# A matmul kernel whose TensorE, VectorE and ScalarE first jump past the end of their programs and back

**Chip, cores, metric.** One core of one Trainium2 chip. The time is the device time of an execution in microseconds; smaller is better. Every execution quoted here was of the fast state by the test that compares runs of one kernel. The experiments ran in three calls on three chips, so each ratio is to the runs of the kernel before in the same call.

## The reference

```python
def reference(x, weight, sub_value):          # x 16 x 512 x 1024, weight 1024 x 768, all float32
    return (np.matmul(x, weight) - sub_value).astype(np.float32)
```

As rows, x is 8192 x 1024: 64 tiles of 128 rows. The core must move 87.03 MB: x, the weights and sub_value in, the result out.

## The kernel before

SyncE issues all transfers in an order fixed by a list. ScalarE casts a tile of x to half precision; the tile is transposed by TensorE (then ScalarE copies it out of PSUM) or, for 18 of 64 tiles, by VectorE; TensorE multiplies with the resident weights; VectorE subtracts sub_value, and the result goes out. TensorE's program is a straight head of four tiles and a loop of ten times six tiles. The other engines run straight through. The parts that matter here:

```python
TRANSFERS = [
    ('x', 0, 1), ('w', 0, 1), ('x', 1, 1), ('w', 1, 1), ...          # cut
    ('s', 48, 8), ('x', 56, 8), ('o', 24, 8), ('o', 32, 8), ('s', 56, 8),
    ('o', 40, 8), ('o', 48, 8), ('o', 56, 5), ('o', 61, 2), ('o', 63, 1),
]
...
    dve.add(lambda: nc.vector.memset(idle_w, 0.0), then=count("idle"))
    dve.add(lambda: nc.vector.memset(idle_x, 0.0), then=count("idle"))
...
    def idle(n):                                     # dummy matmuls, ahead of the first transpose
        pe.add(lambda: nc.tensor.ldweights(idle_w, tile_position=(0, 0)), [(counter["idle"], 2)])
        for _ in range(n):
            pe.add(lambda: loaded_matmul(po_b[:, NPO - 1, 0], idle_w, idle_x, start=True, stop=True))
...
    idle(13)
    cast(0)
    ...                                              # one more dummy, then the first real work:
    transpose_tile(0)
...
    for q in (sp, act, dve, pool):
        q.emit(q.ops)
    if LOOP:
        first, size, times = LOOP                    # (4, 6, 10)
        pe.emit(pe.ops[: marks[first]])
        ends = [marks[first + size * n] for n in range(times + 1)]
        pe.emit_loop([pe.ops[a:b] for a, b in zip(ends, ends[1:])])
        pe.emit(pe.ops[ends[-1] :])
```

## Time and profile before

| | before |
|---|---|
| time, median of the 3 runs that were there at the start | 210.81 us (210.66 to 210.87) |
| span of the profiled run, first to last instruction | 208.9 us |
| TensorE: first dummy, first transpose, end of the last matmul | 1.47, 7.42, 201.65 us |
| last output (384 KB): issue, landing | 202.67, 207.64 us |
| 16 DMA engines on the data queue | 97.9% of the span |

The span is split between two resources that are both nearly full, TensorE (busy for 94% of it) and the DMA engines (97.9%); which of them sets the end is the question of this study. Ends of matmuls are modelled in the profile. The lines that carry the reading stand in the prediction. One view that the prediction did not use is the table of issues (size in KB, then us from issue to landing). Its last three outputs are:

```profile
out_dram<-so_ring SPq DMA_DIRECT2D x1, 1920.0 KB, 10.5
out_dram<-so_ring SPq DMA_DIRECT2D x1, 768.0 KB, 6.6
out_dram<-so_ring SPq DMA_DIRECT2D x1, 384.0 KB, 5.0
```

Note the 5.0 us of the smallest; what it says becomes clear with the experiments.

### The profile page before, as it was taken

What the parts mean: (1) busy time and instruction counts of PE and PEld (TensorE: products, weight loads), DVE (VectorE), ACT (ScalarE), POOL (GpSimd) and SP (SyncE); (2) the same over time, 40 slices, a digit from 0 to 9 for tenths busy, and PEclk for the clock granted to TensorE, in tenths of its full rate; (3) what the DMA queues carried; (4) which work ended last, traced back from release to release, by engine and by line L of the source; (5) the groups of instructions that cost most, each with busy time, mean ns of one, the idle gap of its engine ahead of it and who ended that gap; (6) DMA issues with size and microseconds to landing.
All of it is one profiled execution on the core that took longest, in us unless ns stands there. A gap on an engine that the chain in (4) does not pass through costs nothing.

```text
span 208.9 us, 2609 instructions
## 1 busy us (share of the span) xinstructions
PE 196.8 (94%) x1234; PEld 75.5 (36%) x700; DVE 127.1 (61%) x218; ACT 108.8 (52%) x113; POOL 0.8 (0%) x7
## 2 busy tenths in 40 slices
PE   7999699979999999999999999999999999999960
PEld 0233244323434433443443443443344344334310
DVE  0233235956894795597399389479739938942330
ACT  2555659506673761844645576184574746516300
POOL 1000000000000000000000000000000000000000
PEclk9999999999999999999999999999999999999996
DMA  6999999999999999999999999999999999999993
GB/s 199 420 427 425 435 420 437 436 412 447 425 445 433 419 433 423 452 433 414 445 439 408 442 419 447 430 452 406 438 442 419 428 428 433 433 433 423 418 416 136
DMA packets 5476, 87.08 MB, mean 417 GB/s; under 512 B 608, under 2 KB 608, under 8 KB 1888
## 3 DMA queue, kind: packets, MB, share of 16 engines
q1 hardware_dynamic: 5472, 87.03, 97.9%
q8 instruction: 1, 0.02, 0.0%
q14 instruction: 3, 0.02, 0.0%
HBM read 61.87 MB, written 25.17 MB: 417 GB/s over the span
## 4 chain that ended last, share of the span: by engine, by line
PE 72%; DMA 19%; SPq 4%; ACT 1%; issue 1%; DVE 0%
PE po_b L181 64%; DMA x_ring<-in_x_dram 19%; PE pt_b L318 7%; SPq L281 3%; SPq L245 1%; ACT xt_b L331 0%; DVE so_ring L400 0%; ACT x_b L300 0%; SPq L542 0%; ACT x16p_b L300 0%; SPq L133 0%
## 5 line engine op out<-in xcount | busy, mean ns | idle before, releaser
L181 PE MATMUL po_b<-w_sb,xt_b 128*128 128x384 f16 x704 | 126.0, 326 | 0.5 <-DVE w_sb L248 0.3
L400 DVE TENSOR_TENSOR so_ring<-po_b,so_ring 128x768 f32<-128x768 f32 x64 | 60.6, 956 | 58.3 <-PE po_b L181 39.3
L331 ACT COPY xt_b<-pt_b 128x1024 f16<-128x1024 f16 x44 | 44.5, 1012 | 67.2 <-PE pt_b L318 66.3
L351 DVE STREAM_TRANSPOSE xtp_b<-x16p_b 32x256 f32<-32x256 f32 x144 | 62.7, 435 | 3.2 <-ACT x16p_b L300 1.1
L181 PE MATMUL po_b<-w_sb,xtp_b 128*128 128x384 f16 x320 | 61.3, 326 | 1.3 <-DVE xtp_b L351 1.1
L380 PEld LDWEIGHTS <-xt_b 128*128 128x128 f16 x352 | 34.5, 98 | 58.0 <-issue 54.0
L300 ACT CAST x_b<-x_ring 128x1024 f16<-128x1024 f32 x46 | 47.2, 1048 | 4.0 <-DMA x_ring<-in_x_dram 4.0
L318 PE MATMUL pt_b<-ident,x_b 128*128 128x128 f32 x184 | 47.6, 274 | 1.6 <-ACT x_b L300 1.5
L318 PEld LDWEIGHTS pt_b<-ident,x_b 128*128 128x128 f32 x184 | 25.5, 141 | 46.3 <-issue 36.1
L300 ACT CAST x16p_b<-x_ring 128x1024 f16<-128x1024 f32 x18 | 18.8, 1046 | 14.3 <-DMA x_ring<-in_x_dram 14.3
L380 PEld LDWEIGHTS <-xtp_b 128*128 128x128 f16 x160 | 15.7, 98 | 19.8 <-issue 17.7
L248 DVE CAST w_sb<-so_ring 128x768 f16<-128x768 f32 x8 | 4.1, 556 | 13.1 <-DMA so_ring<-in_weight_dram 13.1
L181 PE MATMUL po_b<-idle_x,idle_w 128*128 128x512 f16 x26 | 9.2, 514 | 1.5 <-DVE idle_x L411 1.5
L331 ACT COPY xtp_b<-pt_b 128x1024 f16<-128x1024 f16 x2 | 2.0, 1012 | 2.3 <-PE pt_b L318 2.3
L300 ACT ACT_TABLE_LOAD x1 | 1.3, 1283 | 0.9 <-SPq L133 0.9
L415 PEld LDWEIGHTS <-idle_w 128*128 128x128 f16 x4 | 0.4, 100 | 1.5 <-DVE idle_x L411 1.5
L410 DVE MEMSET idle_w<- 128x64 uint32 x1 | 0.1, 112 | 1.0 <-SPq L133 1.0
L487 ACT CAST stub<-ident 128x1 f16<-128x1 f32 x2 | 0.4, 195 | 0.0
L170 POOL TENSOR_SCALAR_AFFINE_SELECT ident<-ident 128x128 f32<-128x128 f32 x1 | 0.3, 292 | 0.1
L411 DVE MEMSET idle_x<- 128x256 uint32 x1 | 0.3, 272 | 0.0
L169 POOL MEMSET ident<- 128x128 f32 x1 | 0.2, 204 | 0.5 <-SPq L133 0.5
L464 POOL MEMSET mark<- 128x1 f32 x1 | 0.1, 98 | 24.2 <-ACT xtp_b L331 24.2
(4 smaller groups left out, 0.4 us busy)
## 6 DMA issues: line engine op xcount, KB each, us to landing
so_ring<-in_sub_value_dram SPq DMA_DIRECT2D x7, 3072.0 KB, 24.3
out_dram<-so_ring SPq DMA_DIRECT2D x7, 3072.0 KB, 26.1
x_ring<-in_x_dram SPq DMA_DIRECT2D x5, 4096.0 KB, 23.0
x_ring<-in_x_dram SPq DMA_DIRECT2D x2, 2048.0 KB, 27.6
so_ring<-in_weight_dram SPq DMA_DIRECT2D x4, 768.0 KB, 8.7
x_ring<-in_x_dram SPq DMA_DIRECT2D x1, 3072.0 KB, 28.8
x_ring<-in_x_dram SPq DMA_DIRECT2D x2, 1024.0 KB, 25.2
out_dram<-so_ring SPq DMA_DIRECT2D x1, 1920.0 KB, 10.5
```

Source lines behind the costliest of these rows:

```text
L181: return nc.tensor.add_instruction(mybir.InstMatmult(name=nc.get_next_instruction_name(), engine=full.engine, ins=list(full.ins), outs=lis ...
L245: sp.add(lambda st=st, at=at: nc.sync.dma_start(out=st, in_=w_c[at]), then=(sem, 16))
L248: lambda at=at, r=r, st=st: nc.vector.tensor_copy(out=w_sb[:, at, r], in_=st[:, r]),
L281: sp.add(lambda here=here, there=there: nc.sync.dma_start(out=here, in_=there), waits, (sem, 16))
L300: act.add(lambda: nc.scalar.copy(out=to, in_=x_in), waits, count("cast"))
L318: pe.add(lambda: nc.tensor.transpose(words, from_, ident), waits, count("turn") if last else None)
L331: act.add(lambda: nc.scalar.copy(out=to, in_=pt_b[:, b]), waits, count("evac"))
L351: dve.add(lambda: nc.vector.transpose(xt[b * Q : (b + 1) * Q, :, a * Q : (a + 1) * Q], x16[a * Q : (a + 1) * Q, :, b * Q : (b + 1) * Q],), ...
L380: pe.add(lambda weights=weights: nc.tensor.ldweights(weights, tile_position=(0, 0)), [w for w in waits if w[0] in ready])
L400: dve.add(lambda: nc.vector.tensor_tensor(out=o, in0=po[:, :, :NS], in1=o, op=mybir.AluOpType.subtract), [landed["s", mi], (counter["mul"] ...
L415: pe.add(lambda: nc.tensor.ldweights(idle_w, tile_position=(0, 0)), [(counter["idle"], 2)])
L487: lambda t=t: nc.scalar.copy(out=stub[:, t - n_mt : t - n_mt + 1], in_=ident[:, :1]), [(counter["ident"], 2)], count("cast")
```

## The change

The intent is to have the far end of each long program fetched at the start, instead of while the DMA engines are full of data: in the trace of before, one packet of instructions of 16 KB starts at 35.4 us and three of 8 KB at 57.0, 86.9 and 160.8 us. Three engines make a first turn in which they skip all their work and land behind it, then come back and do it.

```diff
-    for q in (sp, act, dve, pool):
+    engines = OrderedEngineSet([mybir.EngineType.PE, mybir.EngineType.DVE, mybir.EngineType.Activation])
+    for q in (sp, pool):
         q.emit(q.ops)
+    turn = nc.alloc_registers("turn", engines=engines)
+    nc.regs_mov(turn, 0)
+    nc.br("turn_head", engines=engines)
+    with nc.body("turn_head", valid_engines=engines):
+        nc.br_cmp(turn, 0, on_true="past", on_false="work", comp_op="IS_EQ", engines=engines)
+    with nc.body("work", valid_engines=engines):
+        for q in (act, dve):
+            q.emit(q.ops)
         ...                                # TensorE's head and loop, as before
+        nc.br("past", engines=engines)
+    with nc.body("past", valid_engines=engines):
+        nc.regs_alu(turn, turn, 1, op=mybir.AluOpType.add)
+        nc.br_cmp(turn, 2, on_true="turn_head", on_false="rest", comp_op="IS_LT", engines=engines)
+    nc.switch_bb("rest")
```

> **What bounds the kernel now.** I read the page first (busy shares, DMA queues, the chain), then the order of time around the start, then the gaps of TensorE up to 52 us, then a table by stretches.
>
> ```profile
> PE 196.8 (94%) x1234; PEld 75.5 (36%) x700; DVE 127.1 (61%) x218; ACT 108.8 (52%) x113; POOL 0.8 (0%) x7
> q8 instruction: 1, 0.02, 0.0%
> q14 instruction: 3, 0.02, 0.0%
> PE 72%; DMA 19%; SPq 4%; ACT 1%; issue 1%; DVE 0%
> ```
>
> TensorE is busy for 94% of the span, and the chain that ended last is 72% TensorE and 19% a DMA. The two queue lines are the whole traffic of instructions within the span: four packets. In the trace they start at 35.4 us (the one of 16 KB, 1.07 us long) and at 57.0, 86.9 and 160.8 us (8 KB each, 0.31 to 0.33 us).
>
> Where TensorE is the bound is told by stretches (width, then busy time of PE, PEld, DVE, ACT, POOL, clock, DMA share, GB/s):
>
> ```profile
> 26.07:44.77 18.70, 17.61 (x112) 6.79 (x64) 12.29 (x22) 11.05 (x12) 0.00 (x0) 1.00 1.00 426
> 96.80:201.50 104.70, 104.70 (x677) 41.78 (x385) 69.12 (x117) 55.02 (x58) 0.00 (x0) 1.00 1.00 431
> ```
>
> From 52 us to the last matmul TensorE has no idle time at all: 104.70 of 104.70 us. Before, it has. So a delay at the start costs what is left of it after TensorE's waits before 52 us. The start, in order of time (start, length, engine, operation, in brackets the idle time before and what ended it):
>
> ```profile
> 0.90 1.28 ACT L300 ACT_TABLE_LOAD   x1 [0.90 <-SPq L133]
> 1.14 0.27 DVE L411 MEMSET idle_x<- 128x256 uint32 x1
> 1.47 6.12 PE L181 MATMUL po_b<-idle_x,idle_w 128*128 128x512 f16 x14 [1.47 <-DVE idle_x L411]
> 4.96 1.04 ACT L300 CAST x_b<-x_ring 128x1024 f16<-128x1024 f32 x1 [2.77 <-DMA x_ring<-in_x_dram]
> 6.86 1.03 DVE L248 CAST w_sb<-so_ring 128x768 f16<-128x768 f32 x2 [5.44 <-DMA so_ring<-in_weight_dram]
> 7.42 0.60 PE L318 MATMUL pt_b<-ident,x_b 128*128 128x128 f32 x4
> ```
>
> ScalarE idles 2.77 us for the first x, VectorE 5.44 us for the first weights. TensorE does not idle: it fills 1.47 to 7.42 with 14 dummy matmuls, which wait for VectorE's second memset and stand in order ahead of the first transposes. The cast that those need ends at 4.96 + 1.04 = 6.00. So a later start of TensorE, or of VectorE's memsets, moves the transposes at 7.42 one for one; ScalarE's does not until it exceeds its own 2.77 us. These are the gaps after that:
>
> ```profile
> 18.63 2.11 PE L181 MATMUL po_b<-w_sb,xt_b 128*128 128x384 f16 x12 [0.32 <-DVE w_sb L248]
> 23.30 0.44 PE L318 MATMUL pt_b<-ident,x_b 128*128 128x128 f32 x2 [1.47 <-ACT x_b L300]
> 26.07 0.81 PE L181 MATMUL po_b<-w_sb,xtp_b 128*128 128x384 f16 x4 [0.16 <-DVE so_ring L400]
> 44.77 0.81 PE L181 MATMUL po_b<-w_sb,xtp_b 128*128 128x384 f16 x4 [1.09 <-DVE xtp_b L351]
> 51.16 0.81 PE L181 MATMUL po_b<-w_sb,xt_b 128*128 128x384 f16 x4 [0.15 <-ACT xt_b L331]
> ```
>
> A gap is slack only where what ended it does not itself follow TensorE. The following lines tell:
>
> ```profile
> 21.21 1.01 ACT L331 COPY xtp_b<-pt_b 128x1024 f16<-128x1024 f16 x1 [0.91 <-PE pt_b L318]
> 22.20 1.04 ACT L300 CAST x_b<-x_ring 128x1024 f16<-128x1024 f32 x1
> 25.05 2.69 DVE L400 TENSOR_TENSOR so_ring<-po_b,so_ring 128x768 f32<-128x768 f32 x3 [4.62 <-DMA so_ring<-in_sub_value_dram]
> 33.64 1.82 DVE L400 TENSOR_TENSOR so_ring<-po_b,so_ring 128x768 f32<-128x768 f32 x2 [5.90 <-DMA so_ring<-in_sub_value_dram]
> 49.07 1.04 ACT L300 CAST x16p_b<-x_ring 128x1024 f16<-128x1024 f32 x1 [7.60 <-DMA x_ring<-in_x_dram]
> ```
>
> The cast behind the 1.47 us gap stands right behind a copy at 21.21 that TensorE's own transposes released: that gap moves with TensorE and absorbs nothing. The others hang on transfers: 0.32 on the weights; 0.16 on VectorE's subtractions at 25.05, which waited for sub_value; 1.09 on VectorE's transposes, which follow without a break from 33.64, again a landing; 0.15 on the x that landed just before 49.07. Those transfers were issued long before (the x of 49 us at 10.35) and the DMA engines are full, so a start some us later does not move them. Slack: 0.32 + 0.16 + 1.09 + 0.15 = **1.72 us**.
>
> [...] no stall stands beside any of the four[...]. [...] In this trace a compare-and-branch of ScalarE has 33 ns and one of TensorE 174 ns, and the nine jumps back in TensorE's loop leave no gap after the first (whose 1.09 us VectorE explains)[...].
>
> **The change part by part.** It removes no work. Matmuls, casts, transfers, waits and TensorE's loop of ten bodies are the same, in the same order, by the comparison of the two programs. Per engine it adds, before the first useful instruction: one register move, a jump, a compare-and-branch taken to the far end, an add, a compare-and-branch back, a compare-and-branch not taken: six. At the end: an add and a compare-and-branch, at 202.6 us at the latest, while SyncE waits for the last transfers till 206.9; free. GpSimd and SyncE are not touched, so transfers start as before.
>
> (1) Sequencer work: 6 x about 0.1 us = 0.6 us, an estimate from the branch durations above.
>
> (2) Misses. The distances are 333 instructions on TensorE, 229 on VectorE, 157 on ScalarE[...]. The trace does not name the engine of a fetch packet[...]. One miss, estimated from this trace: from SyncE's issue of the first x at 0.94 to its first packet at 1.97 are 1.0 us; the packet itself 0.3 to 1.07 us[...]: about 2 us. TensorE's jumps may hit: its loop goes back 177 instructions after the fetch at 35.4 and no further fetch appears[...].
>
> (3) The delay d of TensorE's start is the larger of its own and VectorE's. No miss: d = 0.6. One: 2.6. Two: 4.6. ScalarE with two, its table load at 5.5, casts at 6.8, 1.8 later than before, but with TensorE's transposes as late as 12 us that is hidden.
>
> (4) Cost = d - 1.72 where positive: 0, 0.9, 2.9 us. At the tail it passes through, as the last matmul, the last subtraction (0.96 us) and the last 384 KB follow each other.
>
> (5) Gain: fetches in the span can move to the start, but none of the four stalls TensorE after 52 us. 0.
>
> I give no miss 0.3, one 0.3, two 0.35, more 0.05 (d about 7, cost 5): 0.27 + 1.0 + 0.25 = 1.5 as the mean. As part of a second miss lies under the clock of another engine's, I take 1.2 us: **212.0 us**.
>
> **Rivals.** *All hidden:* [...] for it speak the four packets alone and the loop's free jumps. Then 210.6 to 211.0 us. *Misses pile up:* [...] the fetch queues behind the x and weight transfers that SyncE has started meanwhile, and a miss takes 3 us; against it, the 16 KB packet under full DMA took 1.07 us. Then d is 7 to 8 and the time 216 us, over 2%. *The warmed end pays:* fetches of 0.3 us at 57, 87 and 161 us vanish[...]; against it, no stall in the bound stretch. Then 210.3 us. *ScalarE becomes the head's bound:* needs three misses there alone.
>
> **Range and chances.** 210.7 to 214.0 us holds the cases of no, one and two misses. Faster by over 2% would need 4.2 us saved where no wait on instructions is seen: 0.01. Slower by over 2% needs d above 5.9 us, three misses or more: 0.08. Within 2%: 0.91.
>
> **What the profile would show.** Step 1 and 2: the first dummy matmul at 1.5 + d, the table load at 0.9 + ScalarE's d, and instruction packets near 1 to 5 us. Step 3: the transposes at 7.42 + d, the first x cast still at about 4.96 unless ScalarE missed twice. Step 4: the gaps at 18.63, 26.07, 44.77 and 51.16 shrink by d together, and only the rest reappears as a later last matmul (201.65 before). I am wrong if the gap at 44.77 closes and the end yet stays, if the continuous stretch from 52 us gets gaps at fetches, or if the start moves by more than 6 us.

Passages on how instructions are fetched and how long a branch takes are cut from this prediction, as no trace or run of this case shows them. The sum itself stands as it was: 0.6 us of sequencer work and about 2 us a miss make d 0.6, 2.6 or 4.6 us, less 1.72 us of slack; the mean over the chances is 1.5 us, of which 1.2 were taken, on 210.8: 212.0 us. Three terms have lost ground to the cuts. Of the 0.1 us a step, what is left to rest on are the 33 and 174 ns of the trace, whose mean is 0.10. Of the 2 us a miss, a few tenths for waiting behind data are cut; 1.0 and 0.3 to 1.07 us are left, 1.3 to 2.1 together. And the count of misses, one on VectorE and perhaps one more on the way back, was the author's assumption: the trace of before did not show it.

## The result, and the profile after

The time did not change: 210.75 us median of 4 runs (210.46 to 211.06) against 210.84 us of before in the same session. The ratio is 0.9998, 95% interval 0.9980 to 1.0015. (Ratios here are the mean time of one kernel's fast runs over that of the other's in the same rounds, so not quite the ratio of the medians.) The result is correct.

Yet the start did move, by nearly what the prediction's case of "two misses" said. The order of time at the start of the changed kernel, to be held against the lines at 0.90, 1.14, 1.47, 4.96 and 7.42 us in the prediction:

```profile
1.77 1.28 ACT L300 ACT_TABLE_LOAD   x1 [1.77 <-issue]
5.63 0.11 DVE L410 MEMSET idle_w<- 128x64 uint32 x1 [5.63 <-issue]
5.91 1.04 ACT L300 CAST x_b<-x_ring 128x1024 f16<-128x1024 f32 x1 [2.85 <-DMA x_ring<-in_x_dram]
6.07 6.09 PE L181 MATMUL po_b<-idle_x,idle_w 128*128 128x512 f16 x14 [6.07 <-DVE idle_x L411]
12.00 0.60 PE L318 MATMUL pt_b<-ident,x_b 128*128 128x128 f32 x4
```

ScalarE is 0.87 us late, VectorE and, through its memsets, TensorE 4.60 us: 6.07 - 1.47. The sequencer records say which engine waited. The register move, jump, add and jump back run from 0.90 to 1.74 us on ScalarE and from 1.05 to 1.99 us on TensorE, without a hole. On VectorE the compare-and-branch starts at 1.04 us and the add behind it at 5.10: 4.06 us for one jump. The way back has no such hole (5.18 to 5.54). So one miss, on VectorE alone, and not two. (A jump is said to miss here if its engine's next sequencer record comes microseconds later and a packet of instructions lies in the hole, as the 8 KB at 3.25 us do here; what that packet brings is called the far page. The other jumps out and back in this trace, which are said to hit, have the next record 0.23 to 0.44 us after their start.)

The instruction packets have moved: in this trace they start at 2.04, 3.25 and 8.30 us (8 KB each) and 3.86 us (16 KB), and none is left later. Before, they were at 35.4, 57.0, 86.9 and 160.8 us.

Next, the gaps of TensorE. Of those that the prediction listed at 18.63, 23.30, 26.07, 44.77 and 51.16 us, one is still shown with a releaser (the view leaves out gaps under 0.15 us; the one of 26.07 is still there, 0.15 us before the matmul at 30.40):

```profile
27.65 0.44 PE L318 MATMUL pt_b<-ident,x_b 128*128 128x128 f32 x2 [1.40 <-ACT x_b L300]
```

That is the one said to move with TensorE; it did, by 4.34 us. Matmul by matmul, the lateness is 4.60 us at the first dummy, 4.10 after the weights' gap, 4.34 to 4.36 after ScalarE's chain, 2.99 after the gap of 44.77, 2.67 after that of 51.16, and 2.39 from 52.2 us to the last matmul. TensorE ends 2.39 us later, 204.04 for 201.65. The last subtraction of each kernel, before and after:

```profile
201.68 0.96 DVE L400 TENSOR_TENSOR so_ring<-po_b,so_ring 128x768 f32<-128x768 f32 x1 [1.64 <-PE po_b L181]
```

```profile
204.08 0.96 DVE L400 TENSOR_TENSOR so_ring<-po_b,so_ring 128x768 f32<-128x768 f32 x1 [1.64 <-PE po_b L181]
```

So 2.4 us of delay reach the last tile, and yet the time is the same. They vanish behind it, in the table of issues of the changed kernel:

```profile
out_dram<-so_ring SPq DMA_DIRECT2D x1, 1920.0 KB, 7.7
out_dram<-so_ring SPq DMA_DIRECT2D x1, 768.0 KB, 3.8
out_dram<-so_ring SPq DMA_DIRECT2D x1, 384.0 KB, 2.3
```

Each output is issued some 2.4 us later and takes 2.7 to 2.8 us less. The 16 parts of the last one landed between 204.95 and 207.64 us before, and between 207.19 and 207.37 us after. Before, the outputs queued behind transfers that were still draining. They did not drain alike: before, thirteen of the sixteen parts had landed by 205.93 us, and the last three, at 207.11 to 207.64 us, set the end. Why these three lag was not tested.

### The profile page after: what moved, and what is told of

It is laid out like the page before. It is cut to its first block, busy times and chain, and to the rows that moved or that the text cites. A ratio compares the mean times of both kernels' runs of the same rounds, so it can differ in the third digit from the quotient of the medians.

```text
span 208.7 us, 2630 instructions
## 1 busy us (share of the span) xinstructions
PE 196.2 (94%) x1234; PEld 75.6 (36%) x700; DVE 127.6 (61%) x218; ACT 108.9 (52%) x113; POOL 0.8 (0%) x7
## 3 DMA queue, kind: packets, MB, share of 16 engines
q1 hardware_dynamic: 5472, 87.03, 97.9%
## 4 chain that ended last, share of the span: by engine, by line
PE 92%; ACT 3%; issue 2%; DVE 1%; DVEq 0%; SPq 0%
PE po_b L181 82%; PE pt_b L318 10%; ACT x_b L300 1%; ACT xt_b L331 1%; ACT xtp_b L331 0%; DVE so_ring L400 0%; DVE idle_x L411 0%; DVE idle_w L410 0%; DVEq L507 0%; DVEq L519 0%; DVEq L518 0%; DVEq L555 0%; DVEq L504 0%; SPq L133 0%
## 5 line engine op out<-in xcount | busy, mean ns | idle before, releaser
L380 PEld LDWEIGHTS <-xt_b 128*128 128x128 f16 x352 | 34.4, 98 | 57.2 <-issue 53.7
```

Source lines behind the costliest of these rows:

```text
L380: pe.add(lambda weights=weights: nc.tensor.ldweights(weights, tile_position=(0, 0)), [w for w in waits if w[0] in ready])
```

## The experiments

**Theory A**: the transfers set the end. At the tail of the kernel before, outputs wait in a backlog of transfers, and TensorE may end some 2.7 us later (5.0 - 2.3) before anyone waits for it. **Theory B**: the late start does cost 2.4 us at the end, and fetching the program early, not between the data, repays them. A third, the prediction's own step, that TensorE's delay passes to the end one for one, has fallen with the result unless something like B repaid it.

### 1 and 2: the delay without any jump

In the kernel before, VectorE writes its buffer of zeros 13 or 20 times more, each write waiting for the one before:

```diff
+    lag = tc.alloc_semaphore("lag")
+    for i in range(13):                     # 20 in the second kernel
+        dve.add(lambda: nc.vector.memset(idle_x, 0.0), [(lag, i)], (lag, 1))
-    dve.add(lambda: nc.vector.memset(idle_x, 0.0), then=count("idle"))
+    dve.add(lambda: nc.vector.memset(idle_x, 0.0), [(lag, 13)], count("idle"))
```

> The kernel before with no far jump at all; VectorE runs 13 more memsets, one behind the other, ahead of TensorE's dummy matmuls, about 0.35 us each, so that TensorE starts near 6.0 us as in the changed kernel. Theory A (the transfers set the end: a backlog of outputs at the tail drains at the same time however late TensorE hands over the last rows): 210.5 to 211.2 us, last matmul near 204, the last 384 KB land 2.3 us after their issue in place of 5.0. Theory B (fetching the program at the start, not in the middle, repays the late start): without the far jumps nothing repays it, so 213.0 to 213.4 us.

Measured: first dummy at 6.56 us (5.09 late), last matmul's end 203.34 us, time 210.83 us, ratio to before 1.0007 (0.9984 to 1.0030). No far jump, instruction packets in the middle as before (38.1, 50.6, 89.5, 143.8 us), and the time is that of before all the same. Theory B is out: nothing was there to repay. The last 384 KB took 3.0 us, not the 2.3 expected: TensorE was 1.7 us late at the end, not 2.4. The memsets took 0.39 us each, not 0.35. The dummies came to their shorter spacing sooner in this execution (see below; the 14 took 4.91 us, 6.12 in before), so the first transpose was 3.9 us late, not 5.1.

> The same with 20 memsets, about 7 us of delay (TensorE's start near 8.4 us). Theory A: in the changed kernel the last 384 KB already take only 2.3 us from issue to landing, about the least a transfer takes, so the reserve ends near a delay of 4.6 us; from there on a further delay passes one for one: 212.8 to 213.5 us. Theory B: 210.8 plus 7 less 2.2 of gaps, 215.3 to 215.8 us. A third theory, that TensorE's delay is absorbed without limit by something else: 210.8 us.

Measured: first dummy at 9.30 us, last matmul's end 206.42, time 213.17 us, ratio 1.0119 (1.0090 to 1.0147), inside theory A's numbers. The reserve is finite: of the 4.8 us by which TensorE ends late, some 2.5 show. The last output has come down to its least:

```profile
out_dram<-so_ring SPq DMA_DIRECT2D x1, 384.0 KB, 2.3
```

### 3 to 7: the backlog taken away

If the backlog hides the delay, the delay must show without it. The last load of sub_value is cut to an eighth of each row, on purpose with a wrong result; 2.75 MB less flow in the last 40 us. No instruction of TensorE changes.

```diff
+            if (kind, at) == ("s", 56):
+                here, there = here[:, :, :96], there[:, :, :96]
```

> Wrong result on purpose: the last load of sub_value (3 MB) brings an eighth of each row, the rest of the rows keeps older numbers; 2.75 MB less to move in the last 40 us, all else as in the kernel before. Theory A: the backlog at the tail is gone, TensorE's end at 201.7 sets the time: 208.0 to 208.6 us. Theory B, or if the end hung on TensorE all along: 210.6 to 210.9 us, for no instruction of TensorE moves.

> The same cut in the changed kernel. Theory A: its last matmul at 204.0 already sets the end, so nothing is gained by the cut: 210.3 to 210.8 us, 2.0 to 2.5 us over the cut kernel without far jumps: the delay comes back to light. Theory B: the two cut kernels have the same time within 0.3 us.

Measured: before with the cut 208.56 us (ratio 0.9898 to before uncut, 0.9877 to 0.9919), with TensorE's end still at 201.91. So in the kernel before the end hung on the transfers. The changed kernel with the cut: 209.88 us (0.9944; 0.9912 to 0.9976), 1.3 us above, less than the 2.0 to 2.5 expected, and with runs from 208.94 to 210.41. I therefore ran both again, with the memset delay as a third.

> The cut kernel before in the same call, as the base: 208.3 to 208.7 us, runs within 0.4 us.

> The cut changed kernel again with more rounds, since its four runs spread over 1.5 us. Theory A: 1.0 to 2.3 us above the cut kernel before in the same call. If the spread comes from the miss (which the timed runs do not show), it stays wide here and is narrow in the kernel with memsets; if it comes from TensorE's slow first matmuls, both are wide.

> The cut load (wrong result on purpose) with the 13 memsets in place of the far jump, TensorE's start near 6.5 us. In the uncut kernel this delay cost nothing (ratio 1.0007). Theory A: without the backlog it costs what reaches TensorE's end, 1.4 to 2.4 us over the cut kernel without delay: 209.8 to 211.0 us. If the cost of the first cut pair (1.3 us) came from the instruction fetches and not from the late start, this one equals the cut kernel without delay within 0.3 us.

Measured: 208.63, 208.94 and 210.53 us; ratios to before uncut 0.9895 (0.9880 to 0.9909), 0.9908 (0.9893 to 0.9922) and 0.9972 (0.9956 to 0.9989). The delay by memsets, free in the uncut kernel, costs 1.9 us here. Two expectations were missed. The base spread over 0.84 us (208.09 to 208.93) where 0.4 was expected, so the spread of the others (0.87 and 1.08 us) doesn't tell the miss from the dummies. And the second run of the cut changed kernel is only 0.3 us above the base, with intervals that overlap. For its profiled execution the reason is in the trace. The last subtraction in the cut kernels without jumps, with jumps the first time, with jumps the second time, and with memsets (the first line is of the repeated base):

```profile
201.69 0.96 DVE L402 TENSOR_TENSOR so_ring<-po_b,so_ring 128x768 f32<-128x768 f32 x1 [1.64 <-PE po_b L181]
```

```profile
204.02 0.96 DVE L402 TENSOR_TENSOR so_ring<-po_b,so_ring 128x768 f32<-128x768 f32 x1 [1.64 <-PE po_b L181]
```

```profile
202.10 0.96 DVE L402 TENSOR_TENSOR so_ring<-po_b,so_ring 128x768 f32<-128x768 f32 x1 [1.64 <-PE po_b L181]
```

```profile
204.48 0.96 DVE L402 TENSOR_TENSOR so_ring<-po_b,so_ring 128x768 f32<-128x768 f32 x1 [1.64 <-PE po_b L181]
```

In the second execution of the same program VectorE's jump took 2.93 us in place of 4.14, and the dummies got fast sooner (the 14 took 5.10 us, 5.97 the first time). TensorE's lateness has these two sources of scatter here, so the timed runs, which leave no trace, can't be put against one TensorE end. The profiled ones can, since the device time of the same execution is known:

| profiled run | TensorE's end | time of that run | difference | last 384 KB, issue to landing |
|---|---|---|---|---|
| before | 201.65 | 210.77 | 9.12 | 5.0 |
| memsets, 13 | 203.34 | 210.47 | 7.13 | 3.0 |
| after | 204.04 | 210.46 | 6.42 | 2.3 |
| memsets, 20 | 206.42 | 212.84 | 6.42 | 2.3 |
| cut, before (first, again) | 201.91, 201.65 | 208.33, 208.09 | 6.42, 6.44 | 2.3, 2.3 |
| cut, after (first, again) | 203.99, 202.07 | 210.41, 208.50 | 6.42, 6.43 | 2.3, 2.3 |
| cut, memsets 13 | 204.44 | 210.89 | 6.45 | 2.3 |

Wherever the last output takes 2.3 us, the least in any of the thirteen traces, the time is TensorE's end plus 6.42 to 6.45 us. Without the cut and without delay it is 9.12: 2.7 us of waiting behind other transfers. The changed kernel's profiled run stands just at the edge of that reserve. Its three other runs took 0.3 to 0.6 us more; what set their end no trace shows.

The prediction held the clock of the dummies as given. The starts of the 14 dummies lie 0.427 us apart at first and 0.216 later, and the slow phase lasts from 3.39 us (the repeated cut base) to 5.95 us (before) in these traces. What ends it no run here shows. The 2.6 us between the two come to 1.26 us for TensorE, since a dummy of the slow phase takes twice the time of a later one (0.427 to 0.216 us): from the same first dummy at 1.47 us, the first transpose starts at 6.16 and at 7.42 us. It fits this scatter that the cut kernel with memsets, which has no miss, has runs from 209.90 to 210.98 us; in the timed runs it was not seen directly.

### 8 to 10: whose jump it is

Only VectorE jumps, the others are emitted as in before:

```diff
-    engines = OrderedEngineSet([mybir.EngineType.PE, mybir.EngineType.DVE, mybir.EngineType.Activation])
-    for q in (sp, pool):
+    engines = OrderedEngineSet([mybir.EngineType.DVE])
+    for q in (sp, act, pool):              # and TensorE's head and loop ahead of the turn
...                                         # cut
```

> Only VectorE jumps past its program and back; TensorE and ScalarE run as in the kernel before. If VectorE's missing far page alone makes the late start: its first memset near 5.1 to 5.7 us, TensorE's first dummy matmul near 6.1, ScalarE's table load at 0.9, two 8 KB instruction packets at 2 to 3.5 us, TensorE's 16 KB packet back in the middle (30 to 42 us). Time by theory A 210.4 to 211.1 us, by theory B (pass-through, or repaid only when all three fetch early) 212 us or more.

Only TensorE and ScalarE jump:

```diff
-    engines = OrderedEngineSet([mybir.EngineType.PE, mybir.EngineType.DVE, mybir.EngineType.Activation])
-    for q in (sp, pool):
+    engines = OrderedEngineSet([mybir.EngineType.PE, mybir.EngineType.Activation])
+    for q in (sp, pool, dve):
...                                         # cut: "work" then emits act alone, and TensorE
```

> TensorE and ScalarE jump, VectorE does not. Both found their far page in the changed kernel (their jump and return took some 0.9 us), so: TensorE's first dummy matmul near 2.0 us (1.5 before), ScalarE's table load near 1.8, no pair of 8 KB packets at 2 to 3.5 us, TensorE's 16 KB packet at 3 to 5 us. Last matmul 201.6 to 202.0, time 210.4 to 211.0 us. If they too wait for a page once VectorE does not lead, the first dummy matmul is past 3 us.

The order of time in each, VectorE alone first:

```profile
0.90 1.28 ACT L300 ACT_TABLE_LOAD   x1 [0.90 <-SPq L133]
5.76 0.11 DVE L410 MEMSET idle_w<- 128x64 uint32 x1 [5.76 <-issue]
6.20 0.10 PEld L415 LDWEIGHTS <-idle_w 128*128 128x128 f16 x1 [6.20 <-DVE idle_x L411]
```

```profile
1.03 0.11 DVE L410 MEMSET idle_w<- 128x64 uint32 x1 [1.03 <-SPq L133]
1.77 1.28 ACT L300 ACT_TABLE_LOAD   x1 [1.77 <-issue]
2.05 5.15 PE L181 MATMUL po_b<-idle_x,idle_w 128*128 128x512 f16 x14 [2.05 <-DVE idle_x L411]
```

VectorE's jump makes the whole late start (its compare-and-branch to the add: 4.19 us); the other two cost 0.6 and 0.9 us. Times: 210.87 us (0.9994; 0.9977 to 1.0010) and 210.80 us (0.9991; 0.9975 to 1.0008), both as theory A has it. The packets tell whose is whose: VectorE alone has 8 KB at 3.38 and 8.44 us, not two at 2 to 3.5 as I had expected, with TensorE's 16 KB back at 33.6 us; the other two have 8 KB at 2.01 and 16 KB at 3.90. In the middle, VectorE alone leaves one packet of 8 KB (89.4 us), the other two leave two (57.2 and 161.0 us). So the page that VectorE waits for is the one packet of 8 KB at 3.38 us, 0.31 us long (3.25 in the changed kernel), and the packet at 2 us belongs to ScalarE, which did not wait for it.

Then all three engines make the trip twice:

```diff
-        nc.br_cmp(turn, 0, on_true="past", on_false="work", comp_op="IS_EQ", engines=engines)
+        nc.br_cmp(turn, 2, on_true="past", on_false="work", comp_op="IS_LT", engines=engines)
-        nc.br_cmp(turn, 2, on_true="turn_head", on_false="rest", comp_op="IS_LT", engines=engines)
+        nc.br_cmp(turn, 3, on_true="turn_head", on_false="rest", comp_op="IS_LT", engines=engines)
```

> All three engines jump to the end and back twice. If the way out misses once and both pages then stay: VectorE's first memset near 6.1 us (5.63 plus 0.5 for a second trip that hits), TensorE's start near 6.5; by theory A, with the reserve used up at 4.6 us of delay, 210.6 to 211.6 us. If each trip loses the far page again, the first memset is near 9.6 us and the time 213.5 to 214.5 us.

Measured: first memset at 6.74 us, 211.12 us (1.0013; 0.9996 to 1.0030). The first jump took 4.49 us; the second, from the start of its compare-and-branch at 5.91 to the add at 6.24, 0.33 us. So neither end of the program had to be fetched again: out and back the second trip took 0.68 us. The memset is 1.11 us later than in the changed kernel: 0.43 from the longer first jump, 0.68 from that second trip (5.91 to 6.59), where I had expected 0.5.

### 11: the first transfer held until VectorE is back

The changed kernel, with one wait more on SyncE:

```diff
+            if (kind, at) == ("x", 0):
+                waits.append((counter["idle"], 1))
```

> The changed kernel with one wait more: SyncE's first transfer waits for VectorE's first memset, so that the page is fetched while no data move. If the miss of 4.0 us was mostly waiting behind the x and weight transfers, it shrinks to some 2.5 us (memset near 4.1, transfers from 4.3); if the fetch itself is that long it stays 4.0 (memset 5.6). Theory A: the transfers now start later by the memset's time plus 0.1 less 0.94, and since they set the end the time grows by all of that: 3.3 us (214.1) to 4.8 us (215.6), although TensorE starts no later than in the changed kernel. Theory B, TensorE alone counting: no more than 211.5 us.

```profile
4.89 0.11 DVE L412 MEMSET idle_w<- 128x64 uint32 x1 [4.89 <-issue]
5.03 0.38 SPq L283 DMA_DIRECT2D x_ring<-in_x_dram  x1
5.33 0.10 PEld L417 LDWEIGHTS <-idle_w 128*128 128x128 f16 x1 [5.33 <-DVE idle_x L413]
```

Measured: 214.75 us, ratio 1.0173 (1.0155 to 1.0191). TensorE starts earlier than in the changed kernel (5.33 for 6.07), yet the kernel is the slowest of all: the first transfer is 4.09 us later than in before (5.03 for 0.94), and the time is 3.8 us longer by the medians. TensorE's end, at 205.67 us, plus 6.43 would give 212.1 for the profiled run; it took 215.62, and its last 384 KB needed 5.8 us. So a late start of the transfers by 4 us goes into the time nearly whole, a late start of TensorE does not. The way there is not so even: landings are 3.9 us late up to 37 us, 3.1 us late from 42 us and up to 4.9 us late at the end, where one part of the last output came 2.06 us after the other fifteen. What makes the lateness grow again was not tested. As to the miss, VectorE's jump took 3.32 us with no data moving. That is less than most (4.06 to 4.49), but more than the 2.93 of one execution with data moving. Whether the transfers lengthen the miss stays open.

No run beat both kernels: every uncut one of this study stayed within 210.3 to 211.6 us or was slower.

## Why the prediction was wrong

It forecast 212.0 us and found 210.75: the direction of every early step was right, the end was not.

- **Step 1, sequencer work 0.6 us**: about right for VectorE, where 4.60 less the jump of 4.06 leaves 0.54 us. ScalarE's trip cost 0.87 us. TensorE's took 0.94 us (1.05 to 1.99); it delayed the first dummy by only 0.58, as that had waited for VectorE's memsets till 1.47 in any case. In the changed kernel the jumps that hit took 0.23 to 0.44 us from start to the next instruction, more than the 0.1 us a step that the prediction took.
- **Step 2, misses of about 2 us, perhaps two**: the term was mis-sized twice over, with errors that cancelled. There was one miss, 4.06 us long. It is not the packet that was mis-sized (0.31 us) but what surrounds it: 2.2 us from the jump to the packet's start (1.04 to 3.25), 1.5 us from its end to the next instruction (3.56 to 5.10). The split varies: in the two cut runs of this program the packets of VectorE and ScalarE start together at 2.0 to 2.1 us and take 0.8 to 2.1 us. The 1.0 us from issue to first packet of a data transfer was a poor stand-in. The way back hit.
- **Step 3, d = 4.6 us** for its heaviest likely case, with TensorE waiting on VectorE's memsets: 4.60 us, by the luck of those two errors. That ScalarE would stay hidden was right too.
- **Step 4, slack 1.72 us**: 2.21 us were absorbed, and in seven traces in which the first transpose is 3.9 to 7.0 us late, TensorE's end is 2.2 us less late. The gap of 1.47 us moved along with TensorE, as argued. The gap at 26.07 did too, which the prediction counted as slack: it gave 0.01 us. The gaps at 44.77 and 51.16 gave 1.26 and 0.32, each 0.17 more than listed, and the matmuls around 52 us another 0.28: waits inside a run of matmuls, which the profile shows as busy time. The weights' gap gave 0.50, of which ScalarE's chain took 0.26 back; about 0.1 went near 33 us.
- **Step 4, "At the tail it passes through"**: this is the step that failed. The prediction reasoned from the order of work (matmul, subtraction, output) and did not ask whether the last output's 5.0 us could shrink. The runs showed that it takes 2.3 us where nothing queues ahead and that 2.7 us of the 5.0 were queueing, a second slack larger than the 2.39 us that arrived. The prediction had noted itself that the DMA engines are full, and the page has them at 97.9% of the span, but it used this for the gaps before 52 us alone. Its own sign of being wrong came true: the gap at 44.77 closed, TensorE's last matmul moved, and the time stayed.
- **"Transfers start as before"**: nearly. In the changed kernel two of SyncE's early issues take longer (1.15 and 1.17 us for 0.43 and 0.45), and landings are 0.9 to 1.2 us late up to 35 us, 0.3 to 0.4 us late from 39 to 154 us, and earlier than before from 185 us on. So about 1 us of lateness of the transfers vanished on the way too; how was not followed. The x of 49 us was issued 4.3 us later (14.62) and landed only 0.38 us later, as the prediction had argued for a full queue.
- **Step 5, no gain**: right; with or without packets in the middle the time is the same.

That 210.75 us lies within the stated range, at its foot, is luck: that end was meant for a start without a miss.

## What to carry to other kernels

A kernel with two full resources can have slack at its tail: before you pass a delay through the last transfer, compare that transfer's time from issue to landing with the least that one of its size takes; here the difference, 5.0 less 2.3 us, was queueing that could shrink. Test which resource sets the end by delaying each by itself; here a first dummy 5 us late (3.9 us at TensorE's first real work) cost nothing, 4 us on the first transfer cost nearly 4. The far jump gained nothing here, where no fetch stalled TensorE, and it cost VectorE 2.9 to 4.5 us at the start. Whether it would pay where a fetch does stall the bound engine was not tested.

## What the runs showed besides

- A jump that misses: on VectorE, over 229 instructions, it took 2.93 to 4.49 us in five traced executions with data moving and 3.32 in one without; in the changed kernel's, 4.06 us for a packet of 0.31. Jumps over 333 instructions on TensorE and 157 on ScalarE did not wait (0.40 and 0.44 us in the changed kernel), nor did the second trip of VectorE (0.33 us).
- The packets of instructions: TensorE's has 16 KB (0.93 us long in the changed kernel, 1.07 in before); VectorE's miss fetched one packet of 8 KB (0.31 us).
- Where TensorE and ScalarE jump, SyncE's issues of two weight transfers take 1.15 and 1.17 us (changed kernel), in place of 0.43 and 0.45 before, and the first x lands at 5.88 us, not 4.93. With VectorE jumping alone the issues take 0.43 and 0.54 us and x lands at 5.31. Which of the two engines does it, and how, was not tested.
- The table by stretches reads a granted clock of 1.00 for 0 to 7.42 us of before, in which the dummies start 0.427 us apart, where those after 7.86 us start 0.216 us apart. The trace's clock record begins at 7.42 us only, and the table counts what has no record as full speed. At the start, the spacing of matmuls is the better witness.
